# The first modulation's weights: half of them streamed through TensorE past silu(c), and chunk 1 of x loaded last

## The chip, the cores and the metric

The kernel runs on one core of one Trainium2 chip. A core has five engines with a queue each: TensorE (PE in the profile, its weight loads PEld), VectorE (DVE), ScalarE (ACT), GpSimd (POOL) and SyncE (SP), which here issues nearly all transfers from HBM. Each queue is worked off in order, and an instruction at its head waits on semaphores that other engines or transfers raise. The metric is the device time of one execution in microseconds (us), the median of several runs.

## The reference

Two decoder layers on x (1024 tokens x 1024 features) with a condition c (1024). Of each layer this matters here:

```python
cond = jax.nn.silu(c)
for layer in range(DEPTH):
    mod = cond @ w_ada[layer] + b_ada[layer]
    shift, scale, gate = jnp.split(mod, 3, axis=-1)
    h = rmsnorm(x, g_pre[layer]) * (1.0 + scale[:, None, :]) + shift[:, None, :]
    y = mixer(h, ...)          # four kinds of attention, gates, one output projection
    x = x + gate[:, None, :] * rmsnorm(y, g_post[layer])
```

So nothing of layer 0's first projection can start before rmsnorm's statistics of x and the first 2 x 1024 columns of `mod` are there. Those columns are a product of a vector of 1024 with a matrix of 1024 x 2048, 8 MB in float32.

## The kernel before, in words

Features lie on partitions, tokens along the free axis, in two chunks of 512 tokens. x comes as 8 tiles of 128 x 512 per chunk (256 KB each). Every large product is computed from high and low halves in the type fp32r: `kstep` (lines 124 to 130) issues three matmuls of 128 x 512 for one slice of 128 features.

The opening is a list of steps, the string PLAN at line 31, worked off in `run`:

- x, y: load chunk 0, chunk 1 of x (line 1172), 8 transfers on SP.
- r, s: statistics of chunk 0, chunk 1. `squares` (line 190 on ACT, 194 on DVE) adds the squares of 8 tiles. `rstd` sums them over partitions with four matmuls that have the data as weights and a column of ones as the moving side (line 205). Eleven small DVE instructions (207 to 213) make the inverse root, and four matmuls (217) spread it over partitions. ACT copies the result out (367).
- A: a quarter of the modulation, called q0 to q3 here: 512 columns, two tiles of shift and two of scale. Eight slices of weights, 128 x 512, are loaded (line 281) into a ring called `raw`. Each is multiplied by its 128 numbers of silu(c), one per partition, and added to `acc`: the first on ACT (286), seven on DVE (283). Then `mod_tiles` sums `acc` over partitions with four matmuls (295), and DVE adds bias and factors (304, 306).
- W: load and split one weight of the first projection into high and low (91 on ACT, 92 on POOL), and give it a PSUM bank. There are five.
- n: pre-norm of those tiles of chunk 0 whose modulation is there, two per quarter (`pre_norm`; DVE 326 and 333, ACT 332, 329 and 91, POOL 92). m: the same for two tiles of chunk 1.
- P: the `kstep`s of all banks and all tiles that are there.

After the list the five banks of chunk 0 are emptied (672 to 674) and those of chunk 1 follow. The order on each engine is not that of the string alone: a scheduler places instructions, and `high_priority` pulls the sums of a quarter and the pre-norms ahead. What stands in the queues below is the built order.

Of the kernel before, what the change touches and what calls it, by code (L numbers as in the profile page):

```python
# [14 lines left out]
AF = mybir.ActivationFunctionType  # L15
ALU = mybir.AluOpType
# [6 lines left out]
C = 512  # L23
# [4 lines left out]

PLAN = "xAWWrnWyPAWnAPWnsAPnnmmmmP"


class Trunk:
# [253 lines left out]
        with self.tc.high_priority(offset=60):  # L288
            self.mod_tiles(l, tiles, a)

    def mod_tiles(self, l, tiles, a):
        nc = self.nc
        p = self.psum("pt")
        for j in range(len(tiles)):
            nc.tensor.matmul(p[:, j:j + 1], a[:, j * 128:j * 128 + 128], self.ones, start=True, stop=True)
        runs = []
        for j, t in enumerate(tiles):
            if runs and t == runs[-1][1] + runs[-1][2] and t % 8:
                runs[-1][2] += 1
            else:  # L300
                runs.append([j, t, 1])
        for j, t, n in runs:
            m = self.mod[l][:, t:t + n]
            nc.vector.tensor_tensor(out=m, in0=p[:, j:j + n], in1=self.v_bada[:, l * 24 + t:l * 24 + t + n], op=ALU.add)
            if t // 8 == 1:
                nc.vector.scalar_tensor_tensor(out=m, in0=m, scalar=1.0, in1=self.v_gpre[:, l * 8 + t - 8:l * 8 + t - 8 + n],
                                               op0=ALU.add, op1=ALU.mult)
            elif t // 8 == 2:
                g = self.v_gpost[:, l * 8 + t - 16:l * 8 + t - 16 + n]
                nc.vector.scalar_tensor_tensor(out=m, in0=m, scalar=0.5, in1=g, op0=ALU.mult, op1=ALU.mult)  # L310
# [847 lines left out]
    def run(self):  # L1158
        nc, I = self.nc, self.I
# [6 lines left out]
        with self.tc.tile_pool(name="early", bufs=1) as early:  # L1166
            xs = [[], []]

            def load_x(ch):
                for kc in range(8):  # L1170
                    x = self.t("t" if (ch, kc) == (1, 7) else "h", [128, C])
                    nc.sync.dma_start(x, I["x"][ch, :, kc])
                    xs[ch].append(x)

            raw = lambda: self.t("raw", [128, C], bufs=10, pool=early)
            ws, banks, done = [], [], []
            rs = {}
            q = 0

            for step in PLAN:  # L1180
                if step in "xy":
                    load_x("xy".index(step))
                elif step in "rs":
                    ch = "rs".index(step)
                    rs[ch] = self.copied(self.rstd(self.squares(xs[ch]), 1024))
                elif step == "A":
                    tiles = [2 * q, 2 * q + 1, 8 + 2 * q, 9 + 2 * q]
                    self.drain(self.ada(0, lambda kc: I["wadaa"][q, kc], tiles,
                                        self.t("acc", [128, C], bufs=2, pool=early), raw))
                    q += 1  # L1190
                elif step == "W":
                    j = first[len(ws)]
                    ws.append(self.weight(j[0], 8, 128, early if len(ws) > 1 else None))
                    banks.append(self.bank(True) if len(banks) < 5 else self.psum("o"))
                    done.append(0)
                elif step == "n":
                    with self.tc.high_priority(offset=60):
                        for kc in range(len(h[0]), min(8, 2 * q)):
                            h[0].append(self.pre_norm(0, kc, xs[0][kc], rs[0]))
                elif step == "m":  # L1200
                    for kc in range(len(h[1]), min(8, len(h[1]) + 2, len(h[0]))):
                        h[1].append(self.pre_norm(0, kc, xs[1][kc], rs[1]))
                else:
                    for n, (w, p) in enumerate(zip(ws, banks)):
                        for kk in range(done[n], len(h[0])):
                            self.kstep(p, w, kk, h[0][kk], kk == 0, kk == 7)
                        done[n] = len(h[0])
            K = len(ws)
            for name in ("mc", "ms"):
                tables.append(self.t("x8", [128, 1024]))  # L1210
                nc.sync.dma_start(tables[-1], I[name])
            late = [first[n][3][0][3](0, banks[n]) for n in range(K)]
            for kc in range(len(h[1]), 8):
                h[1].append(self.pre_norm(0, kc, xs[1][kc], rs[1]))
            for n in range(K):
                p = self.bank(True)
                for k in range(8):
                    self.kstep(p, ws[n], k, h[1][k], k == 0, k == 7)
                late.append(first[n][3][0][3](1, p))
            for f in late:  # L1220
                if f:
                    f()
            self.setup2()
# [214 lines left out]
```

## Time and profile before

| | us |
|---|---|
| median of 3 runs (1373.97 to 1377.67) | 1376.84 |
| the profiled execution | 1375.71 |
| its span in the profile | 1373.9 |
| TensorE busy in it | 1274.9 (93%) |
| TensorE busy in its first 40 us | 13.1 |
| TensorE busy from 80 to 100 us | 19.2 of 20 |
| VectorE busy in the first 80 us | 59.0 |

The rows of a timeline read: start, duration, engine, line, operation, output<-inputs, shape, count, and in brackets the idle time ahead and what ended it. Rows of SPq are transfers being issued. A matmul's duration is its latency; from one start to the next is what it costs TensorE in a stream. An fp32 matmul (not fp32r) appears as two records, so four of them read x8. In the table of windows each engine has its busy time and, in brackets, its instructions; PEclk is the clock that the profile says was granted.

### The profile page before, as it was taken

What the parts mean: (1) busy time and instruction counts of PE and PEld (TensorE: products, weight loads), DVE (VectorE), ACT (ScalarE), POOL (GpSimd) and SP (SyncE); (2) the same over time, 40 slices, a digit from 0 to 9 for tenths busy, and PEclk for the clock granted to TensorE, in tenths of its full rate; (3) what the DMA queues carried; (4) which work ended last, traced back from release to release, by engine and by line L of the source; (5) the groups of instructions that cost most, each with busy time, mean ns of one, the idle gap of its engine ahead of it and who ended that gap; (6) DMA issues with size and microseconds to landing.
All of it is one profiled execution on the core that took longest, in us unless ns stands there. A gap on an engine that the chain in (4) does not pass through costs nothing.

```text
span 1373.9 us, 20797 instructions
## 1 busy us (share of the span) xinstructions
PE 1274.9 (93%) x6940; PEld 1056.0 (77%) x6940; DVE 905.0 (66%) x1963; ACT 732.0 (53%) x1507; POOL 333.4 (24%) x316
## 2 busy tenths in 40 slices
PE   2899999999999999899889999999999999999996
PEld 1678778888777777778767777787888888887885
DVE  5855767777767775787877775767645554555475
ACT  4253226666457677854546554546445555556642
POOL 2243421421332215300103232321212111113400
PEclk9899999999999999999999999999999999999998
DMA  8706685555444543472623221212212121233283
GB/s 281 250 17 211 201 274 190 171 171 157 127 151 135 162 131 116 131 230 100 194 87 94 77 80 54 70 51 86 62 35 81 49 76 54 85 108 116 77 268 116
DMA packets 105132, 175.98 MB, mean 128 GB/s; under 512 B 16688, under 2 KB 25904, under 8 KB 105024
## 3 DMA queue, kind: packets, MB, share of 16 engines
q1 hardware_dynamic: 100512, 172.03, 39.5%
q10 hardware_dynamic: 4512, 2.62, 0.6%
q8 instruction: 54, 0.88, 0.3%
q14 instruction: 54, 0.44, 0.1%
HBM read 131.45 MB, written 31.74 MB: 119 GB/s over the span
## 4 chain that ended last, share of the span: by engine, by line
PE 54%; DVE 19%; DMA 9%; issue 8%; ACT 7%; SPq 2%; POOL 1%; DVEq 0%; POOLq 0%; ACTq 0%
PE pj L127 9%; PE pj L128 9%; PE pj L130 9%; PE S L442 7%; PE pt L501 4%; PE o L511 2%; DMA wr<-in_wout_dram 2%; DVE p L464 2%; PE S L127 2%; PE o L510 2%; PE S L130 2%; PE S L128 2%; DVE pt_l L92 2%; ACT p L466 1%; DVE t L347 1%
## 5 line engine op out<-in xcount | busy, mean ns | idle before, releaser
L127 PE MATMUL pj<-h,wh 128*128 128x512 f32 (+1 forms) x816 | 341.0, 418 | 2.0 <-ACT wh L91 2.0
L128 PE MATMUL pj<-h,wh 128*128 128x512 f32 (+1 forms) x816 | 322.2, 395 | 0.0
L130 PE MATMUL pj<-h,wl 128*128 128x512 f32 (+1 forms) x800 | 315.9, 395 | 1.6 <-DVE wl L92 1.6
L92 POOL TENSOR_TENSOR wl<-wr,wh 128x512 fp32r<-128x512 f32 x126 | 165.4, 1322 | 473.6 <-ACT wh L91 429.0
L466 ACT ACTIVATE p<-p,sm 128x128 f32<-128x128 f32 (+3 forms) x192 | 148.8, 775 | 140.4 <-DVE sm L464 137.9
L92 DVE TENSOR_TENSOR pt_l<-pt,pt_h 128x512 fp32r<-128x512 f32 (+1 forms) x232 | 147.0, 635 | 107.7 <-ACT pt_h L91 106.0
L442 PE MATMUL S<-qk,qk 96*128 96x512 f32 (+5 forms) x720 | 174.7, 344 | 21.5 <-DVE sm L464 12.4
L91 ACT ACTIVATE pt_h<-pt 128x512 fp32r<-128x512 f32 (+1 forms) x232 | 127.7, 552 | 100.3 <-PE pt L501 97.2
L130 PEld LDWEIGHTS pj<-h,wl 128*128 128x128 f32 x800 | 151.0, 189 | 34.0 <-DVE wl L92 3.1
L127 PEld LDWEIGHTS pj<-h,wh 128*128 128x128 f32 (+1 forms) x816 | 154.3, 189 | 20.1 <-ACT wh L91 2.9
L442 PEld LDWEIGHTS S<-qk,qk 128*128 128x128 f32 (+1 forms) x720 | 120.6, 189 | 63.4 <-DVE sm L464 27.7
L128 PEld LDWEIGHTS pj<-h,wh 128*128 128x128 f32 (+1 forms) x816 | 154.3, 189 | 16.6 <-DVE h L92 0.2
L91 ACT ACTIVATE wh<-wr 128x512 fp32r<-128x512 f32 x165 | 101.3, 622 | 118.4 <-PE S L128 38.7
L501 PE MATMUL pt<-ident,p 128*128 128x128 f32 x840 | 134.3, 275 | 3.7 <-DVE p L945 2.8
L501 PEld LDWEIGHTS pt<-ident,p 128*128 128x128 f32 x840 | 101.1, 140 | 27.0 <-DVE p L945 4.4
L464 DVE CUSTOM_DVE_ANT_0 p<-S,mask 128x640 f32<-128x640 f32 (+7 forms) x128 | 96.0, 750 | 33.8 <-PE S L442 33.0
L510 PE MATMUL o<-pt_h,v 128*128 128x256 f32 (+1 forms) x408 | 106.6, 281 | 1.5 <-ACT pt_h L91 1.0
L511 PE MATMUL o<-pt_l,v 128*128 128x256 f32 (+1 forms) x408 | 102.6, 286 | 5.5 <-DVE pt_l L92 5.1
L348 POOL TENSOR_TENSOR t<-t,rs 128x512 f32<-128x512 f32 x26 | 36.5, 1402 | 238.5 <-DMA t<-t 159.6
L511 PEld LDWEIGHTS o<-pt_l,v 128*128 128x128 f32 x408 | 77.3, 189 | 15.7 <-DVE pt_l L92 10.3
L510 PEld LDWEIGHTS o<-pt_h,v 128*128 128x128 f32 x408 | 77.2, 189 | 9.6 <-ACT pt_h L91 3.4
L464 DVE CUSTOM_DVE_ANT_0 p<-S,x 128x128 f32<-128x128 f32 (+3 forms) x64 | 48.2, 753 | 25.2 <-PE S L446 21.9
(315 smaller groups left out, 2284.7 us busy)
## 6 DMA issues: line engine op xcount, KB each, us to landing
wr<-in_wod_dram SPq DMA_DIRECT2D x80, 256.0 KB
wr<-in_wout_dram SPq DMA_DIRECT2D x68, 256.0 KB
ad<-in_wadab_dram SPq DMA_DIRECT2D x41, 256.0 KB
wr<-in_wev_dram SPq DMA_DIRECT2D x38, 256.0 KB
raw<-in_wadaa_dram SPq DMA_DIRECT2D x32, 256.0 KB
ogd<-t SPq DMA_DIRECT2D x32, 256.0 KB
t<-t SPq DMA_DIRECT2D x106, 64.0 KB
t<-rd SPq DMA_DIRECT2D x48, 128.0 KB
```

Of the source, the lines that this page charges most:

```text
L91: nc.scalar.activation(hi, src, AF.Copy)
L92: (lo_eng or nc.vector).tensor_tensor(out=lo, in0=src, in1=hi.bitcast(F32), op=ALU.subtract)
L127: nc.tensor.matmul(p, w[0][:, k, :m], h[0], start=first, stop=False)
L128: nc.tensor.matmul(p, w[0][:, k, :m], h[1], start=False, stop=last and w[1] is None)
L130: nc.tensor.matmul(p, w[1][:, k, :m], h[0], start=False, stop=last)
L348: nc.gpsimd.tensor_tensor(out=s, in0=s, in1=self.rs[:, cs], op=ALU.mult)
L442: nc.tensor.matmul(dst, a, k[:, s], start=(n == 0), stop=(n == len(q) - 1 and not more))
L464: nc.vector.tensor_tensor_reduce(out=P[:, :n], in0=S[:, :n], in1=add, scale=-scale, scalar=init, op0=ALU.add, op1=ALU.min, accum_out=nm)
L466: nc.scalar.activation(P[:, :n], P[:, :n], AF.Exp, bias=nm, scale=-1.0, accum_out=l)
L501: nc.tensor.transpose(pt[:, n * 128:n * 128 + 128], b, self.ident)
L510: nc.tensor.matmul(o[:, qcols], w, hi[:, cols], start=start, stop=False)
L511: nc.tensor.matmul(o[:, qcols], w, lo[:, cols], start=False, stop=stop)
```

## The change

Three things. First, the list of steps is another: chunk 0's statistics directly behind its load, then four times a quarter of modulation, a weight, the pre-norms and the `kstep`s, and chunk 1's load behind the fourth quarter. Second, a quarter is now made by `ada_first`: slices 0 to 3 of the weights are the moving side of an fp32 matmul whose stationary side is one column of silu(c). Their sum is a row of 512 in one partition of PSUM, which ACT copies to SBUF. Slice 4 is scaled on ACT, and slices 5 to 7 are added on DVE. `mod_tiles` then sums over partitions as before, with a second matmul per tile that turns a piece of the row into a column. Third, the ring `raw` has 11 buffers in place of 10.

```diff
-PLAN = "xAWWrnWyPAWnAPWnsAPnnmmmmP"
+PLAN = "xrAWnAWPnAWPnAWPnyWPsmmmmP"
...
+    def ada_first(self, l, w, tiles, a, row, raw):
+        nc = self.nc
+        p = self.psum("o")[:1]
+        for kc in range(8):
+            r = raw()
+            nc.sync.dma_start(r, w(kc))
+            if kc < 4:
+                nc.tensor.matmul(p, self.sc[:, kc:kc + 1], r, start=kc == 0, stop=kc == 3)
+                if kc == 3:
+                    nc.scalar.activation(row, p, AF.Copy)
+            elif kc > 4:
+                nc.vector.scalar_tensor_tensor(out=a, in0=r, scalar=self.sc[:, kc:kc + 1], in1=a,
+                                               op0=ALU.mult, op1=ALU.add)
+            else:
+                nc.scalar.activation(a, r, AF.Copy, scale=self.sc[:, kc:kc + 1])
+        with self.tc.high_priority(offset=60):
+            self.mod_tiles(l, tiles, a, row)
...
         for j in range(len(tiles)):
-            nc.tensor.matmul(p[:, j:j + 1], a[:, j * 128:j * 128 + 128], self.ones, start=True, stop=True)
+            s = slice(j * 128, j * 128 + 128)
+            if row is not None:
+                nc.tensor.matmul(p[:, j:j + 1], row[:, s], self.ones[:1], start=True, stop=False)
+            nc.tensor.matmul(p[:, j:j + 1], a[:, s], self.ones, start=row is None, stop=True)
...
-            raw = lambda: self.t("raw", [128, C], bufs=10, pool=early)
+            raw = lambda: self.t("raw", [128, C], bufs=11, pool=early)
...
-                    self.drain(self.ada(0, lambda kc: I["wadaa"][q, kc], tiles,
-                                        self.t("acc", [128, C], bufs=2, pool=early), raw))
+                    self.ada_first(0, lambda kc: I["wadaa"][q, kc], tiles, self.t("acc", [128, C], bufs=2, pool=early),
+                                   self.t("row", [1, C], bufs=1, pool=early), raw)
```

The built order shows where this stands in the queues. The lines of the changed program are its own: 299 is the matmul on a slice of weights, 301 the copy of the row, 316 and 317 the sums of a quarter over partitions, 303 and 306 what 283 and 286 were. First TensorE's queue from the start of the program, before:

```order
L295 MATMUL pt_132<-ones,acc_107 128x1 [waits DVE_49]
L295 MATMUL pt_132<-ones,acc_107 128x1 x3
L205 MATMUL pt_184<-ones,t_161 128x1 x4
L217 MATMUL pt_201<-ident,sm_189 128x128 [waits DMAHW1_49,DVE_49,PE_49]
L217 MATMUL pt_201<-ident,sm_189 128x128 x3
L127 MATMUL S_150<-h_209,wh_140 128x512 [waits Activation_49]
```

and now:

```order
L299 MATMUL o_156<-raw_157,sc 1x512 [waits DMAHW2_49,DVE_49]
L205 MATMUL pt_130<-ones,t_107 128x1 [waits DVE_49]
L205 MATMUL pt_130<-ones,t_107 128x1 x3
L299 MATMUL o_156<-raw_160,sc 1x512 [waits DMAHW3_49]
L299 MATMUL o_156<-raw_163,sc 1x512 [waits DMAHW4_49]
L299 MATMUL o_156<-raw_166,sc 1x512 [waits DMAHW5_49]
L217 MATMUL pt_147<-ident,sm_135 128x128 [waits DMAHW1_49,DVE_49]
L316 MATMUL pt_182<-ones,row_155 128x1 [waits Activation_49]
L317 MATMUL pt_182<-ones,acc_154 128x1
...
L217 MATMUL pt_147<-ident,sm_135 128x128 x3
L299 MATMUL o_218<-raw_219,sc 1x512 [waits DMAHW4_49]
...
L127 MATMUL S_204<-h_206,wh_194 128x512 [waits Activation_49]
```

Four matmuls on slices, and the eight of the sums in place of four, stand ahead of the first `kstep`; four more slices, of the next quarter, stand there too. The second place is TensorE's queue where chunk 0 of the first projection ends and chunk 1 begins. Before, the sums of chunk 1's squares (`t_404`) stand far inside chunk 0's matmuls, and their spreading as well:

```order
L130 MATMUL o_307<-h_314,wx_298 128x512
L205 MATMUL pt_427<-ones,t_404 128x1 [waits PE_49]
L205 MATMUL pt_427<-ones,t_404 128x1 x3
L127 MATMUL pj_392<-h_209,wx_382 128x512 [waits Activation_49]
...
L217 MATMUL pt_444<-ident,sm_432 128x128 x3
L130 MATMUL pj_392<-h_394,wx_383 128x512
```

Now they stand behind the last matmul of chunk 0 (`pj_499`) and directly ahead of the first of chunk 1 (`o_770`):

```order
L130 MATMUL pj_499<-h_468,wx_490 128x512
L205 MATMUL pt_571<-ones,t_548 128x1 [waits DVE_49,PE_49]
L205 MATMUL pt_571<-ones,t_548 128x1 x3
L217 MATMUL pt_588<-ident,sm_576 128x128 [waits DVE_49,PE_49]
L217 MATMUL pt_588<-ident,sm_576 128x128 x3
L127 MATMUL o_770<-h_596,wx_415 128x512 [waits Activation_49]
```

The third place is SP's queue. Chunk 1 of x is now issued behind all 32 slices of weights, and seven of its eight tiles behind both tables of cosines and sines (`mc`, `ms`) as well:

```order
L297 DMA raw_400<-in_wadaa_dram 128x512 [waits DMAHW7_49,PE_49]
L107 DMA wr_417<-in_wev_dram 128x512 [waits DMAHW0_49,Pool_49]
L107 DMA wr_421<-in_wev_dram 128x512 [waits DMAHW1_49,Pool_49]
L1194 DMA t_487<-in_x_dram 128x512 [waits DMAHW2_49]
L107 DMA wr_491<-in_wev_dram 128x512 [waits DMAHW3_49,Pool_49]
L1233 DMA x_146_639<-in_mc_dram 128x1024 [waits DMAHW4_49]
L107 DMA wr_495<-in_wev_dram 128x512 [waits DMAHW5_49,DMAHW0_49,Pool_49]
L1233 DMA x_147_641<-in_ms_dram 128x1024 [waits DMAHW6_49]
L1194 DMA h_473<-in_x_dram 128x512 [waits DMAHW7_49]
```

Before, those eight transfers stood inside the second quarter, seven of them together ahead of its last slice.

More of the change, by code (lines that the diff above doesn't have):

```diff
@@ L289, in ada, with mod_tiles @@
             self.mod_tiles(l, tiles, a)
-    def mod_tiles(self, l, tiles, a):
+    def ada_first(self, l, w, tiles, a, row, raw):
[15 more added lines that the diff above has]
+            self.mod_tiles(l, tiles, a, row)
+    def mod_tiles(self, l, tiles, a, row=None):
         nc = self.nc
```

## The prediction, made before the changed kernel was run

> **What bounds the kernel now.** I read the table of windows first, to see where TensorE is not the bound, and then the timeline of that stretch.
>
> ```profile
> 0.00:10.00 10.00, 0.00 (x0) 0.00 (x0) 2.61 (x10) 4.04 (x7) 0.20 (x4) 1.00 0.73 220
> 10.00:20.00 10.00, 0.72 (x4) 0.72 (x4) 8.60 (x12) 5.10 (x8) 1.27 (x1) 1.00 0.93 342
> 20.00:30.00 10.00, 5.35 (x23) 5.00 (x23) 4.89 (x17) 3.59 (x6) 5.62 (x6) 1.00 0.77 231
> 30.00:40.00 10.00, 7.05 (x18) 4.72 (x17) 9.48 (x12) 7.50 (x13) 3.40 (x3) 1.00 1.05 389
> 40.00:50.00 10.00, 6.18 (x21) 5.08 (x20) 8.37 (x13) 3.42 (x7) 3.41 (x3) 0.66 0.67 234
> 50.00:60.00 10.00, 8.01 (x41) 6.38 (x41) 7.76 (x12) 1.02 (x3) 4.12 (x3) 0.96 0.73 224
> 60.00:70.00 10.00, 10.00 (x45) 8.25 (x44) 7.47 (x18) 1.65 (x3) 1.77 (x1) 0.86 0.49 184
> 90.00:100.00 10.00, 10.00 (x45) 8.07 (x44) 0.75 (x1) 2.32 (x5) 3.02 (x3) 1.00 0.17 52
> 100.00:300.00 200.00, 195.94 (x1027) 162.68 (x1026) 133.18 (x271) 91.54 (x186) 62.22 (x59) 1.00 0.63 200
> ```
>
> From 90 us on TensorE (first column after the length) has hardly a gap, 4 us in the 200 that follow 100. So what the opening gains or loses arrives at the end nearly whole. In the first 60 us it is busy for 27.3 and idle for 32.7. The timeline says for what it waits:
>
> ```profile
> 9.96 3.88 DVE L194 TENSOR_TENSOR t<-t,t 128x512 f32<-128x512 f32 x5 [1.71 <-ACT t L190]
> 12.74 0.72 ACT L286 ACTIVATE acc<-raw,sc 128x512 f32<-128x512 f32 x1
> 13.76 5.47 DVE L283 SCALAR_TENSOR_TENSOR acc<-raw,sc,acc 128x512 f32<-128x512 f32 x7
> 27.25 0.60 ACT L367 ACTIVATE t<-pt 128x512 f32<-128x512 f32 x1 [3.56 <-PE pt L217]
> 27.88 2.43 DVE L326 SCALAR_TENSOR_TENSOR h<-h,mod,t 128x512 f32<-128x512 f32 x2 [2.13 <-ACT t L367]
> 43.83 1.83 PE L295 MATMUL pt<-ones,acc 128*128 128x1 f32 x8 [3.82 <-DVE acc L283]
> 56.39 1.02 PE L295 MATMUL pt<-ones,acc 128*128 128x1 f32 x8 [1.40 <-DVE acc L283]
> 69.09 0.95 PE L295 MATMUL pt<-ones,acc 128*128 128x1 f32 x8
> ```
>
> The four L295 rows (the first, at 19.28, is below) are the four quarters. At 43.83 and 56.39 TensorE stood idle for DVE's sums `acc`; at 69.09 it was no longer idle, only late in its own queue. Chunk 1 follows, and ACT is its pace:
>
> ```profile
> 75.71 0.72 ACT L332 ACTIVATE h<-h,mod 128x512 fp32r<-128x512 f32 x1 [0.30 <-DVE h L326]
> 85.19 0.62 ACT L91 ACTIVATE h<-t 128x512 fp32r<-128x512 f32 x1
> 86.25 0.50 PE L127 MATMUL S<-h,wh 128*128 128x512 f32 x1 [0.48 <-DVE qk L674]
> ```
>
> At 86.25 TensorE has done 138 of the opening's 240 `kstep` matmuls (chunk 0's 120, and 18 of the first bank of chunk 1), and from there it runs on. At 0.23 us each it has 144 at 87.6. That is the **yardstick**: when has the changed kernel done chunk 0 and one bank of chunk 1?
>
> **What the change takes away.** DVE has 12 of the 28 multiply-adds left:
>
> ```profile
> L283 DVE SCALAR_TENSOR_TENSOR acc<-raw,sc,acc x28: 737/752/1755, 13.8 to 66.5; 128x512 f32<-128x512 f32 x28
> ```
>
> 16 x 0.752 = 12.0 us less, and chunk 1's squares no longer stand between the quarters. DVE then has per quarter three of these, three pre-norm instructions of the same length and three small ones: 5 us, and the waits at 43.83 and 56.39 go. What is late next is TensorE itself, which I price now.
>
> **What it adds to TensorE.** The nearest rows to a 1x512 fp32 matmul are fp32 with 128 and with one moving column, least/median/most:
>
> ```profile
> L217 PE MATMUL pt<-ident,sm x144: 270/276/552, 25.2 to 1364.8; 128*128 128x128 f32 x144
> L205 PE MATMUL pt<-ones,t x128: 163/251/353, 21.0 to 1024.1; 128*128 128x1 f32 x128
> ```
>
> (270 - 163) / 127 = 0.84 ns per column and record; 512 columns x 2 records = 0.87 us, against 0.23 for an fp32r matmul of the same width. That is at full clock. At the start the clock is half, whatever the PEclk column says, which has 1.00 there:
>
> ```profile
> 19.28 1.86 PE L295 MATMUL pt<-ones,acc 128*128 128x1 f32 x8 [19.28 <-DVE acc L283]
> 25.17 2.05 PE L217 MATMUL pt<-ident,sm 128*128 128x128 f32 x8 [2.32 <-issue]
> 34.31 0.63 PE L130 MATMUL S<-h,wl 128*128 128x512 f32 x1
> 34.74 0.63 PE L127 MATMUL S<-h,wh 128*128 128x512 f32 x1
> 39.16 0.39 PE L127 MATMUL pj<-h,wx 128*128 128x512 f32 x1
> 39.39 0.39 PE L128 MATMUL pj<-h,wx 128*128 128x512 f32 x1
> 59.95 0.63 PE L130 MATMUL pj<-h,wx 128*128 128x512 f32 x1
> 60.37 0.63 PE L127 MATMUL pj<-h,wx 128*128 128x512 f32 x1
> 62.83 0.40 PE L127 MATMUL pj<-h,wx 128*128 128x512 f32 x1
> 63.08 0.39 PE L128 MATMUL pj<-h,wx 128*128 128x512 f32 x1
> 69.90 0.92 PE L217 MATMUL pt<-ident,sm 128*128 128x128 f32 x6
> ```
>
> Starts are 0.43 apart at 34 and 0.23 at 39, and 0.42 apart again at 60, just behind the sums of 56.39, until they are 0.25 apart at 62.83. Sums of a quarter cost 1.86 at the half clock and 0.95 to 1.02 at the full one; now doubled, 3.7 and 1.95. A slice costs 1.75 and 0.87. Added in all: 16 x 0.87 + 4 x 0.98 = 17.8 us at full clock, which the 32.7 idle us before 60 could hold. But the queue is in order, so I walk it.
>
> Transfers first. The starts of SP's issues show the landing pace, as each waits for the one eight before:
>
> ```profile
> 12.67 0.33 SPq L107 DMA_DIRECT2D wr<-in_wev_dram  x1
> 13.32 0.33 SPq L107 DMA_DIRECT2D wr<-in_wev_dram  x1
> 13.99 0.33 SPq L107 DMA_DIRECT2D wr<-in_wev_dram  x1
> ```
>
> 0.66 us per 256 KB, and the first slice lands at 12.6 (ACT took it at 12.74).
>
> 1. Slice 0 runs 12.65 to 14.4. The sums of squares (L205's kind, 1.85) follow to 16.25, DVE having ended its additions at 13.84. Slices 1 to 3, long landed, run to 21.5. ACT copies the row, 0.7: **22.25**. Eleven small DVE steps and three additions between them end at 21.0.
> 2. Sums of q0 3.7 and the rest of L217's kind 1.5, at half clock: **27.45**. The first pre-norm then starts as late as before (27.88); the earlier statistics win nothing.
> 3. Slices of q1: between 4 x 0.87 = 3.5 and 4 x 1.75 = 7.0, depending on when the clock opens. I take 5.5: **33.0**. The first pre-norms need ACT 0.6, DVE 0.7, ACT 3 x 0.65 and POOL 1.3 behind 27.45, that is 32.2, and hide under it.
> 4. From here no engine but TensorE is late. The splitting of weights is priced by
>
> ```profile
> L92 POOL TENSOR_TENSOR wl<-wr,wh 128x512 fp32r<-128x512 f32 x126 | 165.4, 1322 | 473.6 <-ACT wh L91 429.0
> L91 ACT ACTIVATE wh<-wr 128x512 fp32r<-128x512 f32 x165 | 101.3, 622 | 118.4 <-PE S L128 38.7
> ```
>
>    so per quarter POOL has 3 x 1.3 = 4.0 us of work, ACT 0.7 for a slice, 0.7 for the row, 2 x 0.6 and three pre-norm steps of 0.7 = 4.7, the ten transfers 6.6, and TensorE 8 (q1) to 11. The row's copy is a new wait on ACT, for TensorE's slices; behind it stand the next weight's halves and the pre-norms, but TensorE wants these only 6 to 24 matmuls later. So 120 `kstep`s x 0.2315, three sums x 1.95, eight slices x 0.87: 27.8 + 5.85 + 7.0 = 40.6: **73.6**.
> 5. One closing of the clock such as that around 60 (some 3.4 us at half rate) costs 1.7: chunk 0 ends at **75.3**.
> 6. Chunk 1's statistics now stand behind that. TensorE's sums 0.95, DVE's steps 2.2, spreading 0.92, ACT's copy: first DVE pre-norm at +4.85. ACT then has 12 pre-norm and three evicting instructions, as in the 10.1 us from 75.71 to 85.81, the last tile's POOL half 1.3: the first bank ends at +16.5, with 7.4 us of it busy on TensorE. **91.8**.
>
> 91.8 - 87.6 = **+4.2 us**. Loading chunk 1 last is covered, on these numbers: its eight tiles would end some 62 transfers x 0.66 behind the start, at 45, but the tenth piece of weights ahead of seven of them waits in SP's queue for a buffer that POOL frees when it splits the seventh, behind the row of q3, at about 55. A table and seven tiles on, 9 x 0.66, it is 61 to 64; ACT's squares and DVE's additions take until 69, ahead of 75.3. If that cover is gone, each us late is a us. The eleventh buffer of `raw` only keeps a slice for TensorE to be late with; I price it at nothing, since SP would otherwise wait at a place where transfers are 20 us ahead. Against the profiled execution, 1375.7 + 4.2 = 1379.9; it lies 1.1 below the median, so against that 1381.0. Bounds: step 3 from -2.0 to +1.5, step 5 from -1.7 to three closings, +3.4. What these do not hold is below.
>
> **The rivals.** *The clock stays shut under the streams.* A slice uses one column of the array's 128, and around 57 sums that use it little were followed by half clock. Then twelve slices cost 1.75 (from step 3's 5.5 to 7.0, and 8 x 0.88 = 7.0 more), three sums 3.7 (+5.3), the first 24 `kstep`s partly 0.43 (+2.5): +16.3 on top, 1397; half of that, 1389, if the runs of `kstep`s between open it for part. For it: the row at 59.95. Against, only weakly: the fp32 matmuls at 69.90 left it open, with all columns in use.
>
> *It opens with the first stream and stays.* Then steps 1 to 3 end at 28 (POOL's half of the second pre-norm becomes the wait), and 116 x 0.2315 + 12.85 puts chunk 0 at 67.7 to 69.5: 1.6 to 3.4 us gained, 1374.3. For it: the matmuls from 34.31 on, without a gap, had opened it by 39.16. Against: sums standing in each quarter.
>
> [...]
>
> *The other side: a slice costs two fp32r passes, 0.46*, if a moving column costs less with one weight column. From step 2 on 12 x 0.41 = 4.9 less, and 1.2 less in step 1, where DVE's steps then set 21.0: -1.9, and with the open clock -7.4, so 1369 to 1375. It decides from a slice under 0.5 us; the slope above speaks against it.
>
> **How the numbers follow.** The forecast as worked out 0.40, the shut clock 0.25, the open clock 0.22, the cheap slice 0.13. 0.3% is 4.1 us, about what a measurement tells from no change. The first is split by its bounds, 0.24 slower and 0.16 same; the second is slower; the third 0.17 same and 0.05 faster; the fourth 0.09 faster, 0.04 same. Together faster 0.14, same 0.37, slower 0.49. The range goes from 1371, inside the cheap slice, to 1394, inside the shut clock; the forecast's own is 1377 to 1386.
>
> **What would show it.** Slices (1x512 fp32) about 0.87 us apart, 1.75 before some 30 us; TensorE busy from 33 to 75; an idle stretch of about 5 us behind the last matmul of `pj` in chunk 0, ended by a pre-norm; 144 matmuls done near 92. Wrong if slices are half as dear, if the clock stays shut past 45, or if chunk 1's squares come after 75.

## The result and the profile after

The change is slower: 1388.09 us (median of 6 runs, 1386.17 to 1392.46) against 1376.07 (6 runs, 1373.97 to 1378.40), a ratio of 1.009 (95% interval 1.0074 to 1.0106). The profiled execution took 1387.36 with a span of 1385.6, 11.7 more than before.

Nearly all of it arises in the opening. As a marker I take the first sums of line 205 behind the opening's 240 `kstep` matmuls. Timeline of TensorE, before:

```profile
80.56 0.40 PE L127 MATMUL o<-h,wx 128*128 128x512 f32 x1
...
109.93 0.95 PE L205 MATMUL pt<-ones,t 128*128 128x1 f32 x8
```

After, the same view, from the first slice to that marker (L299 is a streamed slice, L316 and L317 the doubled sums of a quarter):

```profile
13.49 1.87 PE L299 MATMUL o<-raw,sc 128*1 128x512 f32 x2 [13.49 <-DMA raw<-in_wadaa_dram]
...
26.82 4.70 PE L299 MATMUL o<-raw,sc 128*1 128x512 f32 x8
31.45 0.50 PE L127 MATMUL S<-h,wh 128*128 128x512 f32 x1
...
34.81 0.38 PE L317 MATMUL pt<-ones,acc 128*128 128x1 f32 x2 [1.18 <-DVE acc L303]
...
38.17 0.63 PE L128 MATMUL S<-h,wh 128*128 128x512 f32 x1
38.60 0.63 PE L130 MATMUL S<-h,wl 128*128 128x512 f32 x1
...
40.44 4.72 PE L299 MATMUL o<-raw,sc 128*1 128x512 f32 x8
53.45 3.59 PE L299 MATMUL o<-raw,sc 128*1 128x512 f32 x8
56.97 0.50 PE L127 MATMUL S<-h,wh 128*128 128x512 f32 x1
...
59.26 0.38 PE L317 MATMUL pt<-ones,acc 128*128 128x1 f32 x2
59.57 0.38 PE L316 MATMUL pt<-ones,row 1*128 1x1 f32 x2
...
79.14 0.95 PE L205 MATMUL pt<-ones,t 128*128 128x1 f32 x8
82.45 1.13 PE L217 MATMUL pt<-ident,sm 128*128 128x128 f32 x8 [2.36 <-DVE sm L213]
85.94 0.80 PE L127 MATMUL o<-h,wx 128*128 128x512 f32 x1 [2.36 <-ACT h L354]
...
98.41 0.39 PE L127 MATMUL S<-h,wh 128*128 128x512 f32 x1
...
120.57 0.95 PE L205 MATMUL pt<-ones,t 128*128 128x1 f32 x8
```

The marker is 10.6 us later (120.57 against 109.93). Behind it the two spans are alike: 1264.0 us before (1373.9 - 109.93), 1265.0 after. The prediction's yardstick, chunk 0 and one bank of chunk 1, is reached at 98.4 instead of 87.6: +10.8, where +4.2 was forecast.

The rows show two stretches. From 31.45 to 79.14 chunk 0 is worked off almost without a gap (one wait of 1.18 us), and it ends 1.4 us earlier than before, where chunk 1's first matmul starts at 80.56. Then come chunk 1's statistics, and the first bank of chunk 1 ends 19.3 us behind chunk 0; before, as many matmuls took 7.0 (80.6 to 87.6). The table of windows, after, shows it (TensorE is the first column behind the length):

```profile
70.00:80.00 10.00, 10.00 (x49) 8.26 (x47) 2.62 (x4) 0.98 (x2) 0.00 (x0) 1.00 0.31 122
80.00:90.00 10.00, 4.82 (x16) 2.92 (x15) 7.59 (x18) 5.94 (x10) 2.25 (x2) 0.68 0.00 1
90.00:100.00 10.00, 6.94 (x26) 4.38 (x25) 8.31 (x11) 7.61 (x14) 7.00 (x6) 0.97 0.00 0
```

Between 80 and 100 TensorE is busy for 11.8 of 20 us (4.82 + 6.94). The other engines' rows, after, tell what it waits for (timelines of DVE, ACT and POOL):

```profile
67.60 5.33 DVE L194 TENSOR_TENSOR t<-t,t 128x512 f32<-128x512 f32 x6 [0.35 <-ACT t L190]
80.12 0.17 DVE L207 TENSOR_SCALAR pt<-pt 128x4 f32<-128x4 f32 x1 [7.19 <-PE pt L205]
...
83.61 0.60 ACT L389 ACTIVATE t<-pt 128x512 f32<-128x512 f32 x1 [12.64 <-PE pt L217]
84.24 2.08 DVE L348 SCALAR_TENSOR_TENSOR h<-h,mod,t 128x512 f32<-128x512 f32 x3 [1.94 <-ACT t L389]
...
86.90 2.43 DVE L348 SCALAR_TENSOR_TENSOR h<-h,mod,t 128x512 f32<-128x512 f32 x2
89.26 1.82 DVE L355 SCALAR_TENSOR_TENSOR h<-h,mod,h 128x512 fp32r<-128x512 f32 x1
...
95.09 1.46 POOL L701 TENSOR_TENSOR t<-t,t 128x512 f32<-128x512 f32 x1 [0.23 <-ACT t L694]
96.52 1.26 POOL L92 TENSOR_TENSOR h<-t,h 128x512 fp32r<-128x512 f32 x1
```

DVE has added up chunk 1's squares by 72.9. But their sums over partitions stand in TensorE's queue behind the last `kstep` of chunk 0, so DVE is idle for 7.2 us and ACT for 12.6. TensorE keeps them waiting first, and then waits for them.

### The profile page after: what moved, and what is told of

The parts are those of the page before. It is cut to its first block, busy times and chain, and to the rows that moved or that the text cites. A ratio compares the mean times of both kernels' runs of the same rounds, so it can differ in the third digit from the quotient of the medians.

```text
span 1385.6 us, 20898 instructions
## 1 busy us (share of the span) xinstructions
PE 1298.2 (94%) x7004; PEld 1061.2 (77%) x7004; DVE 893.5 (64%) x1947; ACT 734.0 (53%) x1511; POOL 331.6 (24%) x316
## 4 chain that ended last, share of the span: by engine, by line
PE 44%; DVE 13%; ACT 6%; DMA 6%; issue 6%; POOL 1%; SPq 1%; DVEq 0%; POOLq 0%; ACTq 0%
PE pj L127 8%; PE pj L128 8%; PE pj L130 8%; PE S L464 6%; PE pt L523 4%; PE o L533 2%; DVE p L486 2%; PE o L532 2%; DVE pt_l L92 1%; DMA wr<-in_wout_dram 1%; ACT p L488 1%; PE S L127 1%; PE S L130 1%; PE S L128 1%; DMA t<-wd 1%
## 5 line engine op out<-in xcount | busy, mean ns | idle before, releaser
L464 PE MATMUL S<-qk,qk 96*128 96x512 f32 (+5 forms) x720 | 174.2, 343 | 19.2 <-DVE sm L486 10.6
L128 PEld LDWEIGHTS pj<-h,wh 128*128 128x128 f32 (+1 forms) x816 | 154.4, 189 | 16.5 <-DVE h L92 0.2
```

The source lines that it names most:

```text
L128: nc.tensor.matmul(p, w[0][:, k, :m], h[1], start=False, stop=last and w[1] is None)
L464: nc.tensor.matmul(dst, a, k[:, s], start=(n == 0), stop=(n == len(q) - 1 and not more))
```

## The experiments

The marker column below is the start of the same row as above, in the one profiled execution of each kernel. Each ratio is against runs of the kernel before beside it on the same chip; so two kernels with different neighbours are compared by their ratios rather than by their medians. A profiled execution need not be a typical one: e3's is the shortest of four, e8's the longest of ten.

| kernel | median us (runs) | ratio, 95% interval | marker us |
|---|---|---|---|
| before (beside the change) | 1376.07 (6) | 1 | 109.9 |
| the change | 1388.09 (6) | 1.009, 1.0074 to 1.0106 | 120.6 |
| e1: order alone | 1386.27 (4) | 1.009, 1.0057 to 1.0124 | 120.6 |
| e2: streaming alone | 1388.77 (4) | 1.0111, 1.0086 to 1.0135 | 123.0 |
| e3: chunk 1 loaded a quarter earlier | 1388.26 (4) | 1.0106, 1.0066 to 1.0145 | 115.6 |
| e4: two slices per quarter | 1386.92 (4) | 1.0093, 1.0069 to 1.0118 | 119.8 |
| e5: the change, 38 idle matmuls first | 1383.48 (6) | 1.0062, 1.0040 to 1.0084 | 118.2 |
| e6: before, 38 idle matmuls first | 1385.30 (6) | 1.0076, 1.0054 to 1.0098 | 114.4 |
| e7: e3, e4, e5, and squares on POOL | 1388.37 (4) | 1.0091, 1.0068 to 1.0113 | 122.6 |
| e8: before, squares on POOL | 1375.97 (10) | 1.0009, 0.9994 to 1.0024 | 112.1 |
| e9: the change without chunk 1's statistics | 1376.89 (10) | 1.0000, 0.9981 to 1.0018 | 104.1 |
| e10: before without them | 1373.71 (4) | 0.9962, 0.9947 to 0.9977 | 103.7 |
| e11: before, chunk 0's statistics first | 1378.10 (10) | 1.0006, 0.9991 to 1.0020 | 112.4 |
| e12: the change, chunk 1's sums earlier | 1384.93 (6) | 1.0067, 1.0042 to 1.0091 | 118.8 |

### e1 and e2: the two halves of the change, each alone

e1 is the kernel before with the new list, e2 the change with the old one; the diff of e2 is that of e1 turned round.

```diff
-PLAN = "xAWWrnWyPAWnAPWnsAPnnmmmmP"
+PLAN = "xrAWnAWPnAWPnAWPnyWPsmmmmP"
```

> The new list of steps with the old way of making the modulation: all eight slices of a quarter on ACT and DVE, none through TensorE. Theory (the loss is TensorE's own work in the opening, slices and doubled sums and the half clock, plus chunk 1's statistics standing behind chunk 0): DVE then has some 8.3 us per quarter (7 x 0.77 + 3 x 0.75 + 0.6) and brings the fourth quarter at about 49; 79 matmuls of chunk 0 follow it, so chunk 0 ends near 69 and the first bank of chunk 1 19 us later, at 88: 0 to +2 us against the kernel before. Rival (loading chunk 1 last and its statistics behind chunk 0 cost all of it, the streaming nothing): +10 to +12 as in the whole change. Second rival (the new list is good and only the streaming is bad): -5 or better.

> The streaming of four slices of each quarter through TensorE with the old list of steps, where chunk 1's load and statistics stand between the quarters. Theory: DVE is relieved of 12 us and TensorE has room in the first 60 us; the statistics of chunk 1 stay hidden, so the tail of 19.3 us behind chunk 0 shrinks to some 9: -4 to +2 us against the kernel before. Rival (the streaming's TensorE work is what costs): +5 to +11.

Both missed: each half alone costs as much as the whole (12 and 14 us), so the two are not terms of a sum. e1 came in its first rival's +10 to +12, but its reason, that the streaming costs nothing, does not fit e2, which is above even its own rival's +11. TensorE's timeline of e1:

```profile
61.41 1.02 PE L295 MATMUL pt<-ones,acc 128*128 128x1 f32 x8 [2.28 <-DVE acc L283]
...
78.27 0.95 PE L205 MATMUL pt<-ones,t 128*128 128x1 f32 x8
```

With the new order chunk 0 ends at 78.27 though DVE still makes all the additions and TensorE waits for it in each quarter (1.08, 1.03 and 2.28 us). With the streaming it is 79.14. So here the streaming takes those waits away and puts as much of TensorE's own work in their place: from 20 to 80 us TensorE is busy for 46.8 us in e1 and for 58.6 in the change, and chunk 0 ends within 1 us of the same time. In both, chunk 1's first bank follows late, by 20.2 and 19.3 us. And e2's:

```profile
46.34 0.59 PE L317 MATMUL pt<-ones,acc 128*128 128x1 f32 x2 [6.81 <-DVE acc L303]
```

In the old order chunk 1's tiles are loaded ahead of the second quarter's last slices, and its squares stand between the additions on DVE. Three additions a quarter are not late by their length but by what stands ahead of them: TensorE waits 6.8 us there (before, 3.8), and does its slices besides. This is argued from the rows; no run changes that place alone.

### e3 and e4: an earlier load, fewer slices

e3 moves chunk 1's load and statistics a quarter ahead, e4 streams two slices per quarter instead of four.

```diff
-PLAN = "xrAWnAWPnAWPnAWPnyWPsmmmmP"
+PLAN = "xrAWnAWPnAWPynAWPnsWPmmmmP"
```

```diff
-            if kc < 4:
+            if kc < 2:
...
-            elif kc > 4:
+            elif kc > 2:
```

> The changed kernel with chunk 1's load put ahead of the fourth quarter's slices and its statistics ahead of the last weight; nothing else moved. Theory: of the 19.3 us between the last matmul of chunk 0 and the end of the first bank of chunk 1, in which TensorE is busy for 7.4, up to 11 go; TensorE's part of the loss (chunk 0 ending at 79 where the balance needs about 68) stays: 1388 - 8 to 11, so 1377 to 1380, about the kernel before. Rival (chunk 1's tail is paced by ACT and DVE anyway, wherever the statistics stand): 1386 to 1388.

> The changed kernel with two slices of each quarter through TensorE in place of four (the third on ACT, five on DVE). Theory: TensorE is the bound between 31 and 79 us, so eight slices of 0.88 us at full clock come off it, 6 of them behind 31 us plus what the half clock doubled: 5 to 8 us faster than the change, 1380 to 1383. Rival (DVE or the transfers set the pace there, slices are covered): no difference, 1387 to 1389.

e4 met its rival. Eight slices less, 7 us of TensorE at full clock, bring chunk 0's end forward by 1.4 us only (77.78). TensorE then waits for others: 2.8 us for DVE's steps of chunk 0's statistics (up to 19.97), 2.0 in three waits for POOL's halves between 32 and 44, and 1.5 for DVE's last additions (57.60). e3 does take the stretch behind chunk 0 away, and the marker comes 5 us earlier, but a new wait stands in the fourth quarter. Its timeline:

```profile
63.19 0.58 PE L317 MATMUL pt<-ones,acc 128*128 128x1 f32 x2 [3.56 <-DVE acc L303]
```

Chunk 1's squares now stand ahead of the last quarter's additions on DVE. The profiled execution is the shortest of e3's four (1384.12), so the 5 us are at its best; the others reach 1393.13. Their times go with the mean granted clock: 0.986 and 0.985 in the two of 1384, 0.980 and 0.978 in those of 1392 and 1393. On the median e3 is no better than the change, against what was expected.

### e5 and e6: is it the clock?

38 bf16 matmuls of 128 x 512 at the head of TensorE's queue, whose result nothing reads, keep it busy from 1.5 to 12.2 us in e5 and to 11.8 in e6.

```diff
+        p = self.psum("S")[:, :C]
+        for i in range(38):
+            nc.tensor.matmul(p, self.mask[:, :128], self.mask[:, :C], start=True, stop=True)
```

> The changed kernel with 38 bf16 matmuls of 128x512 on a tile of ones at the head of TensorE's queue, in the 12 us in which it has nothing to do; their sums are not used. Theory (a part of the loss is the half clock in the opening): slices 0 to 3, the sums of squares and the first quarter's sums run at full clock, 0.88 us per slice in place of 1.76, the first matmul of chunk 0 starts at 27 to 29 us in place of 31.45: 2 to 4 us faster than the change, 1384 to 1386, and less spread between runs. Rival (the pace there is DVE's, ACT's and the transfers', the clock is no matter): 1387 to 1389.

> The kernel before with the same 38 matmuls at the head of TensorE's queue. Theory: its TensorE waits for DVE's sums until 56 us, so an open clock at 12 us, shut again by the time its first work comes at 19, is worth nothing: -1 to +0.5 us. If it gains 3 us or more, the half clock costs the kernel before as much as the change, and it is no part of the difference.

e5 is 4.6 us below the change by the medians, 0.5 below the range expected. By the ratios it is some 4 us, and their intervals overlap, so the gain is not clear of the noise; and the smaller spread that was expected did not come (7.7 us between its runs, 6.3 in the change). e6 did not come as expected: +10. What its rows show first is that, with the added matmuls, the order built on TensorE and DVE is another. Its DVE timeline:

```profile
44.44 9.32 DVE L194 TENSOR_TENSOR t<-t,t 128x512 f32<-128x512 f32 x6
53.69 5.46 DVE L287 SCALAR_TENSOR_TENSOR acc<-raw,sc,acc 128x512 f32<-128x512 f32 x7
```

Chunk 1's squares now stand in one block ahead of the third quarter's additions, and TensorE waits 5.56 us for these (before, 1.40), about the 4.4 us that the marker is later. The other six arise between 134 and 604 us. Up to 3.4 of them go with the clock: the table of windows of e6 has it at half from 152.2 to 155.7 and from 312.7 to 316.1, where the kernel before has 1.00. What caused these closings, and the rest, stay open. Since e5's order differs from the change's too, its 4.6 us aren't shown to be the clock's alone.

### e7 and e8: the squares' additions on POOL

```diff
-                nc.vector.tensor_tensor(out=acc, in0=acc, in1=s, op=ALU.add)
+                (eng or nc.vector).tensor_tensor(out=acc, in0=acc, in1=s, op=ALU.add)
...
-                    rs[ch] = self.copied(self.rstd(self.squares(xs[ch]), 1024))
+                    rs[ch] = self.copied(self.rstd(self.squares(xs[ch], nc.gpsimd if ch else None), 1024))
```

> A version meant to beat both: two slices of each quarter through TensorE, chunk 1's load ahead of the fourth quarter's slices and its statistics ahead of the last weight, the seven additions of its squares on POOL in place of DVE, and the 38 matmuls at the head that open the clock. Theory: in the run with the statistics early TensorE waited from 59.6 to 63.2 for the fourth quarter's additions, queued on DVE behind the squares of chunk 1; with these on POOL and eight slices less, all of the opening's matmuls are done near 105 to 110 (before 109.9): 1370 to 1377. Rival (POOL's pieces of the weights are then late, 9 us of additions ahead of them, and the clock shuts again): 1380 or more.

> The kernel before with the seven additions of chunk 1's squares on POOL in place of DVE; nothing else. Theory (DVE's queue is what the opening of the kernel before waits for: sums of q1 at 43.83, q2 at 56.39): 5 us come off DVE between 36 and 43 us, and the kernel gets 2 to 5 us faster, 1370 to 1372.5. Rival (POOL then splits the weights late, and TensorE waits for these instead): 0 to +3.

Both missed, and came where their rivals had them. In e7 (TensorE's timeline) POOL is late itself, and the quarter behind it too:

```profile
62.79 1.87 PE L205 MATMUL pt<-ones,t 128*128 128x1 f32 x8 [4.24 <-POOL t L194]
69.02 0.58 PE L321 MATMUL pt<-ones,acc 128*128 128x1 f32 x2 [4.36 <-DVE acc L307]
```

In e8 the wait at the second quarter's sums shrinks from 3.8 to 2.6 us, but the marker is no earlier (112.1). With a ratio of 1.0009, moving the squares' additions to POOL saves the kernel before nothing that these runs can tell.

### e9 and e10: what chunk 1's statistics cost in each kernel

```diff
-                    rs[ch] = self.copied(self.rstd(self.squares(xs[ch]), 1024))
+                    rs[ch] = rs[0] if ch else self.copied(self.rstd(self.squares(xs[ch]), 1024))
```

> The change, but chunk 1 is normalised with chunk 0's statistics: its squares, additions, sums and spreading are left out, so the output is not the reference's. Theory: the change's quarters end 1.5 us earlier than before (79.1 against 80.6), and what costs is the 19.3 us from there to the end of the first bank of chunk 1, against 7.0 before, since the statistics wait for chunk 0's end in the queues. Without them the pre-norms run under chunk 0, the first bank ends 6 to 9 us behind chunk 0, at 85 to 88, and the time is 10 to 13 us less than the change's: 1374 to 1378. Rival: most of the 19.3 are the pre-norms and evictions on ACT, which stay behind chunk 0's end; only the five us from the sums of squares to the first pre-norm go: 1382 to 1384.

> The kernel before, with the same part left out (chunk 1 is normalised with chunk 0's statistics). Theory: before, the statistics are nearly free for TensorE, as they end long before chunk 0 does; but DVE's seven additions stand ahead of the second quarter's last slice, where TensorE waits 3.8 us, and the sums of squares stand among the kstep matmuls (0.95 and 1.2 us). So 1 to 5 us less than before: 1370 to 1374. Rival: the statistics cost the kernel before as much as the change (10 or more us): 1364 or less; then the change does not lose by them.

e9 settles the main point. Without chunk 1's statistics the change is 11.2 us faster and equals the kernel before. Both times came as expected; e9's first bank of chunk 1 ends at 81.8, earlier than the 85 to 88 expected. The table of windows of e9, to be read beside the change's above:

```profile
70.00:80.00 10.00, 10.00 (x45) 8.17 (x44) 6.33 (x8) 8.89 (x16) 8.57 (x7) 1.00 0.00 1
80.00:90.00 10.00, 10.00 (x45) 8.09 (x44) 0.97 (x2) 2.33 (x5) 2.85 (x3) 1.00 0.17 52
```

TensorE has no gap at all here. DVE, ACT and POOL do chunk 1's pre-norms between 70 and 80, under the rest of chunk 0, so neither pre-norms nor evictions were the tail's cause: its rival is out. In the kernel before the same cut is worth 1.7 us by the medians and 5.2 by the ratio (the runs of the kernel before in the same rounds were longer than its median). So the statistics cost the change 11 to 12 us and the kernel before 2 to 5: their work is the same, its place is not. (e9 takes the work out altogether; e12 below moves only its place.)

Two things stay open. e9's marker is 16.5 us earlier than the change's, and only 11 arrive at the end. And e9 and e10 have the marker within 0.4 us, but e9 is 0.4% slower; it falls back by 5 us between 124 and 593. Up to 3.4 of these go with the clock, which e9's profile has at half from 160.1 to 163.5 and from 586.8 to 590.2, and e10's does not; the rest is not explained.

### e11 and e12: the place of the statistics in the queues

e11 is the kernel before with chunk 0's statistics (r) ahead of the first quarter. e12 is the change with chunk 1's sums pulled ahead, 18 `kstep` matmuls for line 205 and 6 for line 217, all else in its order.

```diff
-PLAN = "xAWWrnWyPAWnAPWnsAPnnmmmmP"
+PLAN = "xrAWWnWyPAWnAPWnsAPnnmmmmP"
```

```diff
-                    rs[ch] = self.copied(self.rstd(self.squares(xs[ch]), 1024))
+                    sq = self.squares(xs[ch])
+                    if ch:
+                        with self.tc.high_priority(offset=60):
+                            rs[ch] = self.copied(self.rstd(sq, 1024))
+                    else:
+                        rs[ch] = self.copied(self.rstd(sq, 1024))
```

> The kernel before, with chunk 0's statistics put ahead of the first quarter in the list of steps, as the change has them, and nothing else moved. In the queues the sums of squares then stand ahead of the first quarter's sums. Theory: the first pre-norm no longer waits for 11 small DVE steps behind the sums at 19.28 and starts 3 to 5 us earlier; the later quarters are paced by DVE's additions and take most of it back: 1371 to 1375, 0 to 4 us less. Rival: the order of the list moves other instructions too, and the time is above 1377.

> The change, with chunk 1's sums of squares (four L205 matmuls) 18 kstep matmuls earlier in TensorE's queue and the spreading matmuls (L217) 6 earlier, both ahead of chunk 0's end; the order on ScalarE and VectorE is the same. In the change the additions end at 72.9 but the sums stand behind chunk 0 and start at 79.14. Theory (the tail is a matter of where the statistics stand in the queue): the sums start near 75.0, the spreading near 78.7, the first pre-norm near 80.5 instead of 84.2; the first bank of chunk 1 ends 3.7 to 6 us earlier (the upper end if the shorter idle stretch keeps the clock open), and the time is 1382 to 1384.5. Rival: behind the statistics something else holds chunk 1 up (the evictions of chunk 0, which ACT and POOL share with the pre-norms); the first bank ends less than 1.5 us earlier and the time is 1386.5 to 1388.5.

e11 gains nothing, where up to 4 us were expected (its ratio is 1.0006): the sums run at 13.56, but the spreading matmul waits until 24.42 (8.99 us for DVE), since DVE's small steps stay behind the first quarter's additions in its queue.

e12 is 3.2 us below the change, 0.4 above the range expected; the intervals of the two ratios overlap, so by the times alone this gain is not clear of the noise. TensorE's timeline of e12:

```profile
60.73 0.63 PE L127 MATMUL S<-h,wh 128*128 128x512 f32 x1
61.16 0.63 PE L128 MATMUL S<-h,wh 128*128 128x512 f32 x1
...
77.08 0.95 PE L205 MATMUL pt<-ones,t 128*128 128x1 f32 x8
...
80.75 1.05 PE L217 MATMUL pt<-ident,sm 128*128 128x128 f32 x8
...
84.16 0.51 PE L127 MATMUL o<-h,wx 128*128 128x512 f32 x1 [0.97 <-ACT h L354]
```

Chunk 0 ends at 83.0 and the first bank of chunk 1 at 96.6: 13.6 us between them instead of 19.3. But chunk 0 ends 3.9 later. 1.7 of that are the sums and the spreading, which now lie ahead of its end; and in this execution the clock was shut from 59.3 to 66.1 (`kstep`s 0.43 apart), which is worth 3.4. In the change's profile the same stretch ran at full clock (the sums 0.31 apart at 59.26), with the same queue up to there. Against these stands a start that was earlier by chance: up to 57 us e12 runs 1.0 us ahead, as its first slice starts at 12.60 and not at 13.49. So the bank is 1.8 us earlier in the profile; at the change's clock and without that head start it would be 4.2, inside the 3.7 to 6 expected. The other runs of e12 reach from 1378.76, at a mean clock of 0.990, to 1388.82, at 0.981.

No version that does the whole work beats the kernel before.

## Why the prediction was right, and where its sizes were off

The direction and the mechanism held: slower, with chunk 1's statistics left standing behind chunk 0. The size did not: +4.2 us were forecast and 12.0 measured. The time lies inside the stated range, but above the 1377 to 1386 that the forecast's own terms allowed; the range held it because it reached into the rival of the shut clock, which is not what happened, and that is luck. In the prediction's balance chunk 0 ends 5.3 us earlier than before (75.3 against 80.6) and pays for more than half of a tail that is 9.5 longer (16.5 against 7.0). Measured, chunk 0 ends 1.4 earlier and the tail is 12.3 longer. The time is 7.1 us above the forecast, and these steps carry it:

| step | predicted | measured |
|---|---|---|
| 1, row of the first quarter copied | 22.25 | ACT starts at 22.40, 0.59 long |
| 2, statistics spread | 27.45 | 26.82 |
| 3, slices of the second quarter done | 33.0 | 31.45 |
| 4 and 5, from there to chunk 0's end | 42.3 | 47.7 |
| 6, from there to the first bank of chunk 1 | 16.5 | 19.3 |
| yardstick | 91.8 | 98.4 |

- **The price of a slice** was right: four in 3.52 us behind 53.45 is 0.88 each at full clock, where 0.87 was worked out. At the start it is 1.87 for one. The cheap slice is out.
- **Steps 1 to 3** were close, and the first pre-norm came at 27.56, hardly earlier than before (27.88), as foreseen: the earlier statistics win nothing. Step 2 met its time by two errors that cancel: the row was copied 0.7 later, and the sums, priced at 3.7 for a half clock, ran at the full one, 0.31 apart from 23.04, in 2.5.
- **Step 4** was too small. Doubled sums cost 0.31 us per matmul, whether 128 partitions are summed or one is turned round (59.26 to 59.57 to 59.88), so 2.5 per quarter and not 1.95: +1.6 in three. The wait at 34.81 for the second quarter's additions was not foreseen: +1.2. DVE had waited 1.18 us for a slice to land, and its three additions took 3.71 us where the next quarters' take 2.8.
- **Step 5** allowed 1.7 for one closing of the clock. The change's profile has one in this stretch, from 35.9 to 42.7; at half rate that is 3.4. What is left of the 5.4, some 1 us, is put down to small spacing where the form changes (0.34 from one start to the next at 31.45 and 56.97, 0.32 at 50.24, for 0.23 in a stream).
- **Step 6** has the right shape: the first pre-norm on DVE at +5.1 (forecast +4.85). The rest took 14.2 instead of 11.65. In the rows, two stretches on DVE beside POOL's splits (87.29, 1.49 long, and 89.24, 1.28) are slow (86.90 and 89.26: 4.25 us where the same three instructions take 2.15), and an evicting product of POOL (95.09, 1.46) stands ahead of the last tile's half. The clock was at half as well from 83.7 to 90.5 (0.68 in the row of 80 to 90 above), so the seven `kstep`s there stand 0.43 apart or more; it probably cost little, since TensorE still waits for pre-norms behind it, last 1.26 us for POOL ahead of 97.83. All this is only argued from the rows: none of the runs changed these.
- **"Loading chunk 1 last is covered"** held as worded and was beside the point. The additions ended at 72.9 (forecast 69), ahead of 79.1; but the cover that matters is TensorE's queue. The prediction took the statistics' place behind chunk 0 as given, and so priced the idle time right in kind; what that place costs by itself, 11 to 12 us, is shown by e9.
- **The idle stretch** behind the last matmul of `pj` was forecast at about 5 us, ended by a pre-norm. There are two waits of 2.36 us, around the spreading at 82.45, and a pre-norm (ACT, line 354) ends the second.

Of the rivals, the shut clock gave 1389 in its milder form, near the measured time, but for another reason: the clock did not stay shut under the slices. In the change's profile it is at half through the first slices (1.74 each from 17.09 to 22.30) and open behind them (the sums 0.31 apart from 23.04). Then it shuts three times up to 100 us, by the table of windows cut fine: from 25.7 to 29.1, 35.9 to 42.7 and 83.7 to 90.5. In the kernel before it opens at 38.8 and shuts twice, from 42.2 to 49.1 and 59.3 to 62.7. The clock that opens with the first stream and stays gave 1374.3; it neither opened with that stream nor stayed.

What opens and shuts the clock these runs do not show. In the change it opened at 29.1, 3.4 us after the closing at 25.7 and with slices in flight from 26.82; its first opening, at 22.3, came when slices and sums had run without a gap for 8.8 us, from 13.49. In each of the 14 profiles all changes of PEclk lie whole multiples of 3.41 us apart (in the change at 25.67, 29.08, 35.91 and 42.73). The clock shut at 59.3 in e12 and not in the change, with the same queue up to there. One difference that the rows show is where this grid falls: in e12 the last 3.41 us ahead of 59.3 hold 1.8 us of the one-column sums (from start to start), while in the change a line of the grid, at 59.8, divides these sums into 1.4 and 0.9. That this decides is not shown by these runs.

## What to carry to other kernels

When work is moved off a busy engine, ask which engine the next row in the queue will wait for: here four additions fewer per quarter only changed DVE's lateness into TensorE's, within 1 us. A small reduction that the next stage needs (sums, a root, a spread) costs its whole chain when it stands behind the last of the big work in an in-order queue (11 to 12 us here), and less when it stands in the middle (2 to 5): look in the timeline for engines that idle between its parts. And two halves of a change can each cost the whole, so test both alone before adding terms.

## What the hardware showed that was not expected

- An fp32 matmul with one moving column costs 0.31 us in a row of alternating forms, the same with 128 rows of weights as with one (59.26, 59.57); the eight records of line 205 take 0.95 together, 0.24 each pair.
- The clock can shut in a stretch of such sums with no idle time, for 6.8 us, in one execution of a queue and not in another (e12 at 59.3 and the change, whose queues are alike up to there). It is worth 3.4 us where TensorE is busy throughout, about half of the 6.3 us between the change's shortest and longest run.
- Every closing of the clock that opened again lasts 3.4 us or a whole multiple of it (6.8, 10.2, 13.7, 17.1, 23.9), in all 14 profiles.
- With 10 us of extra matmuls at the idle head of TensorE's queue the kernel before was 10 us slower. About 4 of these go with the order that was built around them, up to 3.4 with two more closings of the clock; the rest is open.
